# One list schedule for two MLPs and the gating unit between them, with the fourth Winograd product one stage later

## The chip, the cores and the metric

The kernel runs on one core of a Trainium2 chip. The metric is device time in microseconds (us): the median of several executions. Beside it stands one profiled execution, whose trace gives the start and length of each instruction. Engines are named as in the profile: PE multiplies matrices (PEld loads its weights), DVE and ACT do elementwise work, POOL issues the accumulating transfers and small scalar work, SP issues the other transfers.

## The reference

A decoder of two layers, 512 tokens, width 1024, everything in float32. Cut to what matters:

```python
for i in range(2):
    sh1, sc1, g1, sh2, sc2, g2 = jnp.split(silu(c) @ ada_w[i] + ada_b[i], 6, axis=-1)
    h = modulate(rmsnorm(x, norm_mix_g[i]), sh1, sc1)
    y = pool_mixer(h, ...) if i == 0 else sgu_mixer(h, ...)
    x = x + g1[:, None, :] * y
    h = modulate(rmsnorm(x, norm_mlp_g[i]), sh2, sc2)
    x = x + g2[:, None, :] * (jnp.square(jax.nn.relu(h @ mlp_w1[i])) @ mlp_w2[i])   # 1024 -> 4096 -> 1024
return rmsnorm(x, final_g)

def sgu_mixer(h, w_in, ln_g, ln_b, w_s, b_s, w_out):      # the gating unit of layer 1
    u, v = jnp.split(gelu(h @ w_in), 2, axis=-1)
    v = layernorm(v, ln_g, ln_b)
    mixed = einsum('hts,bnshc->bnthc', tril(w_s), v in chunks of 128) + b_s
    return (u * mixed) @ w_out
```

## The kernel before, in words

**Numbers.** Each float32 operand is split in two halves of lower precision: ACT writes the high part (`wh`, or the first half of `hb`, `as`, `op`), DVE subtracts it and writes the low part (`wl`, ...). A product is three matmuls: low weights by high data, high by low, high by high (`mm3`). So each 128x1024 weight tile costs ACT one copy, DVE one subtraction, and the two must be done before PE reaches it.

**Both MLPs by Winograd.** The first matrix (w1) is taken in 8 column quads (c, j), c from 0 to 3, j from 0 to 1. Some columns are done plainly (units `f`); the rest, 5 quads of MLP 0 and 7 of MLP 1, take 7 products of block sums instead of 8 (units `s`, products m = 1 to 7). The sums of weight blocks are made in one buffer, tile `tr` (tag `t0` in pool `hx`), as a chain: block (0,0) is loaded and split for m=1, DVE adds a block and it is split for m=5, again for m=6, then POOL issues a transfer that adds block (1,0) in flight, and the result is split for m=4. A product takes 24 matmuls. The order in a quad is 1 5 6 3 7 2 4 (`ORDER`); the first quad of MLP 1 takes 1 2 5 6 3 7, then m=1 of the next quad, then its own 4. Results are evicted to tiles `g` (pool `gq`, 8 buffers); m=4 adds to the PSUM bank that m=1, 6 and 7 have used, so it has to wait until DVE has read m=7 out of it (`g<-g,po`).

The second matrix (w2) goes the same way in units `p` (m, c): `ORDER2`. Its weight sums are chains in tiles `bt`, one for each c, in the homes `HOME`; the additions are transfers that POOL issues (`sum_in`), and its left operands are `op` tiles. The first unit is m=1, c=0.

**The gating unit** in between uses pools of its own (`lp`, `up`, `gp`, `ur`), opened after those of MLP 0 are closed and closed before those of MLP 1 are opened.

**What sets the order.** PE's order is that of the code. A class `Plan` records the instructions of an MLP, then gives out each engine's in an order that a list scheduler finds: it walks a clock, costs each instruction (`cost`), ranks what is ready by how late it may be (`late`), and emits in order of planned start. Costs and lead times are numbers in the code. MLP 0 and MLP 1 are each planned alone (`LEAD`, `LEAD1`); between them the order of DVE and ACT, and of the transfers, comes from the tile framework. An engine executes strictly in the order given: whatever stands behind an instruction that waits, waits too. This holds for SP too, where a transfer waits for its buffer. In the profile the lines tell who emitted: L130 is the plan's, L102 is everything else.

Names: `raw` are weight tiles as loaded (tag `w4`, 3 buffers), `yr` other blocks of the w1 quads, `yb` and `b` blocks of w2, `h32` (short `h` in the profile) the normalized input in float32, `hb` its split halves, `as` split sums of it, `xs` token rows scaled by their norm, `px` their transposes, `ada` weights of the modulation, worked off on DVE beside the rest.

Of the kernel before, what the change touches and what calls it, by code (L numbers as in the profile page):

```python
# [14 lines left out]
P = 128  # L15
D = 1024
# [60 lines left out]
class Plan:  # L77
# [68 lines left out]
    def cost(name, attr, out, ins, kw):  # L146
# [3 lines left out]
        if attr == "dma_start":  # L150
            mb = out[0].free_size() * out[0].partition_size() / 2**18
            return (5.05 * mb, 3.6 + 4.8 * mb) if kw.get("accum_op") else (2.7 * mb, 0.9 + 5.2 * mb)
        if name == "PE":
            n = out[0].free_size()
            t = max((n + 6) / 2400, 0.1117) if ins[0].dtype == F32R else 2 * max((n + 6) / 2400, 0.1055)
            return t, t + 0.165
        if name == "DVE":
            t = n / 960 + 0.065
            return t, t + 0.09
        if name == "ACT":  # L160
            t = n / 1200 + (0.05 if psum else 0.095)
            return t, t + 0.112
        return (0.75, 0.8) if n < 4 else (n / 950 + 0.1, n / 950 + 0.12)
# [39 lines left out]
    def run(self, lead):  # L203
# [37 lines left out]
        for i in range(N - 1, -1, -1):  # L241
            x = min([late[j] - cost[j][1] for j in succs[i] if j > i], default=t + 20)
# [53 lines left out]
        events, now, free, queue = [], 0.0, {e: lead[e] for e in ready}, 0.0  # L296
# [8 lines left out]
        while count < N:  # L305
            moved = True
            while moved:
                moved = False
                for e in ready:
                    if free[e] > now + 1e-9 or e == "SP" and queue > now + self.QUEUED:  # L310
                        continue
# [24 lines left out]
                    if ops[i][1] == "dma_start":  # L336
                        issue = 0.85 if e == "POOL" else 0.35
                        free[e] = now + issue
                        queue = max(queue, now + issue) + cost[i][0]
                        end = max(queue + 1.8, now + cost[i][1]) + 0.7  # L340
                        heapq.heappush(events, (queue - self.QUEUED + 0.01, -1))
                    else:
                        free[e] = now + cost[i][0]
                        end = now + cost[i][1]
                    heapq.heappush(events, (free[e], -1))
                    heapq.heappush(events, (end, i))
# [11 lines left out]
            now, i = heapq.heappop(events)  # L358
# [25 lines left out]
def decoder_kernel(ctx: ExitStack, tc: tile.TileContext, xtok, vecs, fgrow, ada0, ada1, pool_w, w1s, w1, w1f, w1b, w2, w_v, w_u, w_o, wsT, lnp, bs, out):  # L384
# [233 lines left out]
    ordered = ExitStack()  # L618
    ordered.enter_context(tc.manual_schedule(engines={mybir.EngineType.DVE, mybir.EngineType.Activation, mybir.EngineType.SP}))
# [402 lines left out]
    def mlp(i, first, extra, last, ending):  # L1022
# [3 lines left out]
        with (  # L1026
            tc.tile_pool(name="gq", bufs=8) as gq_,
            tc.tile_pool(name="hx", bufs=1) as hx_,
            tc.manual_schedule(engines=ORDERED | ({mybir.EngineType.DVE, mybir.EngineType.Activation, mybir.EngineType.SP} if i and PLAN[1] else set())),
        ):  # L1030
            gq, hx = (plan.pool(p, True) for p in (gq_, hx_))
            plan.on = PLAN[i]
            shift(hx, BASE)
# [98 lines left out]
            def s_prep(u):  # L1132
# [65 lines left out]
            HOME = ((hx, "hx"), (hx, "t0"), (big, "hb00"), (big, "hb10"))  # L1198
# [18 lines left out]
            def block_at(c, r, n):  # L1217
# [7 lines left out]
                elif (c, n) == (2, 1):  # L1225
# [13 lines left out]
            def p_prep(u):  # L1239
# [31 lines left out]
                if m in (1, 5):  # L1271
# [64 lines left out]
            at = len(units)  # L1336
# [35 lines left out]
            if plan.on:  # L1372
# [342 lines left out]
```

## Time and profile before

| | us |
|---|---|
| median of 3 executions (lowest, highest) | 807.11 (806.63, 807.22) |
| the profiled execution, its own time | 808.29 |
| its span, first to last instruction | 806.6 |
| PE busy | 786.3 (97%) |
| DVE busy | 681.1 (84%) |
| ACT busy | 505.0 (63%) |

The stages, by the trace: pooling mixer and the first 7 column blocks of MLP 0 up to 92 us (not planned), w1 of MLP 0 up to 213, w2 up to 360, gating unit up to 496, w1 of MLP 1 up to 656, w2 up to 799, and the end. PE's granted clock is full in nearly all of them (mean 0.999). "Busy" of PE joins matmuls that overlap in its pipeline, so that a pause of less than a matmul's length does not show as idle.

### The profile page before, as it was taken

The page shows a single profiled execution, that of the slowest core. Times are in us where ns is not written, and L with a number is a line of the kernel's source. Part 1 is how long each engine was busy: PE and PEld are TensorE (multiplying, and loading weights), DVE is VectorE, ACT ScalarE, POOL GpSimd, SP SyncE. Part 2 cuts the span into 40 slices and gives each one's busy share as a digit, 9 for nine tenths or more (in the row PEclk, how much of TensorE's full clock was granted, in tenths as well). Part 3 has the DMA queues.
Part 4 walks back from the last instruction along what each step waited for, and adds up shares of the span by engine and source line. Part 5 has one row for each costly group of instructions (what it writes and reads, how often), then busy time and mean ns, then how long its engine had stood idle before and what let it go on. Part 6 is the DMA issues. An engine that isn't in the chain of part 4 may idle for free.

```text
span 806.6 us, 12583 instructions
## 1 busy us (share of the span) xinstructions
PE 786.3 (97%) x4868; PEld 712.8 (88%) x4868; DVE 681.1 (84%) x883; ACT 505.0 (63%) x723; POOL 85.7 (11%) x110
## 2 busy tenths in 40 slices
PE   5999999999999999999999999999999999999996
PEld 5778889999988888888889889999999998888885
DVE  5989798899879997996898976878877987888897
ACT  5486686577756665776334236767776776666662
POOL 4000000010011131010010001001000011113102
PEclk9999999999999999999999999999999999999999
DMA  8989968786999999126756647366776499999802
GB/s 344 417 304 312 348 211 284 248 275 187 337 291 222 236 258 256 67 100 257 243 184 215 216 145 281 134 183 210 195 200 207 137 352 253 265 239 206 220 1 104
DMA packets 46955, 184.40 MB, mean 229 GB/s; under 512 B 5272, under 2 KB 5424, under 8 KB 42672
## 3 DMA queue, kind: packets, MB, share of 16 engines
q1 hardware_dynamic: 36432, 129.33, 43.2%
q0 software_dynamic: 10032, 51.92, 30.7%
q10 hardware_dynamic: 432, 2.36, 0.7%
q8 instruction: 38, 0.62, 0.3%
q14 instruction: 21, 0.17, 0.1%
HBM read 177.28 MB, written 6.30 MB: 228 GB/s over the span
## 4 chain that ended last, share of the span: by engine, by line
PE 87%; DVE 5%; DMA 5%; issue 1%; ACT 1%; SPq 1%; POOLq 0%; DVEq 0%; ACTq 0%
PE pm L130 36%; PE po L130 29%; PE po L102 18%; DMA ada<-in_ada 2%; PE px L102 1%; DMA tr<-in_w1b 1%; DMA x<-in_xtok 1%; PE pq L102 1%; DVE ada L102 1%; DMA raw<-in_w1f 1%; DVE wl L130 1%; DVE wl L102 1%; DVE tr L130 0%; PE pt L102 0%; DVE ht L102 0%
## 5 line engine op out<-in xcount | busy, mean ns | idle before, releaser
L130 PE MATMUL pm<-wh,op 128*128 128x512 f32 x896 | 267.3, 379 | 0.0
L130 PEld LDWEIGHTS pm<-wh,op 128*128 128x128 f32 x896 | 169.3, 189 | 24.1
L130 PE MATMUL po<-hb,wh 128*128 128x256 f32 (+1 forms) x976 | 173.6, 284 | 0.2 <-DVE hb L130 0.2
L130 PE MATMUL pm<-wl,op 128*128 128x512 f32 x448 | 169.8, 379 | 0.0
L130 PEld LDWEIGHTS po<-hb,wh 128*128 128x128 f32 x976 | 150.0, 192 | 2.6 <-DVE hb L130 0.4
L130 PE MATMUL po<-hb,wl 128*128 128x256 f32 (+1 forms) x489 | 136.3, 284 | 2.8 <-DVE g L130 2.2
L130 PE MATMUL po<-as,wh 128*128 128x256 f32 x576 | 97.1, 275 | 0.0
L130 PEld LDWEIGHTS po<-hb,wl 128*128 128x128 f32 x489 | 92.5, 192 | 4.4 <-DVE g L130 2.5
L130 ACT ACTIVATE op<-g 128x1024 fp32r<-128x1024 f32 x56 | 59.3, 1059 | 58.9 <-PE pm L130 52.5
L130 PEld LDWEIGHTS pm<-wl,op 128*128 128x128 f32 x448 | 84.7, 189 | 11.9
L130 DVE TENSOR_TENSOR op<-g,op 128x1024 fp32r<-128x1024 f32 x56 | 68.5, 1223 | 27.2 <-ACT op L130 27.2
L130 PEld LDWEIGHTS po<-as,wh 128*128 128x128 f32 x576 | 87.5, 192 | 0.0
L130 ACT ACTIVATE g<-g 128x512 f32<-128x512 f32 x100 | 60.4, 627 | 31.4 <-DVE g L130 30.5
L130 DVE TENSOR_TENSOR wl<-bt,wh 128x1024 fp32r<-128x1024 f32 x64 | 77.5, 1220 | 2.1 <-ACT wh L130 1.9
L130 PE MATMUL po<-as,wl 128*128 128x256 f32 x288 | 79.3, 275 | 0.0
L130 ACT ACTIVATE wh<-bt 128x1024 fp32r<-128x1024 f32 x64 | 67.0, 1053 | 15.2 <-PE pm L130 13.6
L130 DVE TENSOR_TENSOR wl<-tr,wh 128x1024 fp32r<-128x1024 f32 x48 | 57.9, 1222 | 20.6 <-ACT wh L130 20.5
L102 PE MATMUL po<-hb,wh 128*128 128x512 f32 x240 | 71.6, 380 | 0.0
L130 ACT ACTIVATE wh<-tr 128x1024 fp32r<-128x1024 f32 x48 | 49.9, 1057 | 17.9 <-DVE tr L130 9.9
L102 DVE SCALAR_TENSOR_TENSOR ada<-ada,cb 128x1024 f32<-128x1024 f32 x42 | 50.9, 1220 | 7.6 <-DMA ada<-in_ada 7.4
L130 PEld LDWEIGHTS po<-as,wl 128*128 128x128 f32 x288 | 55.3, 192 | 0.2 <-ACT g L130 0.2
L102 PEld LDWEIGHTS po<-hb,wh 128*128 128x128 f32 x240 | 45.1, 189 | 6.7 <-DVE hb L102 0.6
(216 smaller groups left out, 1259.0 us busy)
## 6 DMA issues: line engine op xcount, KB each, us to landing
ada<-in_ada SPq DMA_DIRECT2D x76, 512.0 KB, 4.9
bt<-in_w POOLq DMA_DIRECT2D x24, 1024.0 KB, 10.8
yr<-in_w1b SPq DMA_DIRECT2D x22, 512.0 KB, 5.8
b<-in_w SPq DMA_DIRECT2D x20, 512.0 KB, 8.5
bt<-in_w SPq DMA_DIRECT2D x16, 512.0 KB, 9.6
tr<-in_w1b SPq DMA_DIRECT2D x12, 512.0 KB, 4.6
raw<-in_w1b SPq DMA_DIRECT2D x12, 512.0 KB, 5.6
wh<-in_ada SPq DMA_DIRECT2D x10, 512.0 KB, 9.7
```

What stands on the lines that cost most here:

```text
L102: return f(*a, **kw)
L130: self.ops.append((name, attr, lambda: f(*a, **kw), out, ins, kw))
```

## The change

Matmuls and their number stay the same. What differs:

1. **One plan.** `plan.on` is set once, before MLP 0, and `plan.run(LEAD)` is called once, at the end. The gating unit and both seams between stages are thereby ordered by the list scheduler too. Pools `gq` and `hx` are opened once for all three; the gating unit's tiles (`lnt`, `wsbs`, `u`, `gt`) are `g` buffers, `ur` is the home `hx`, and the scaled rows `xs` are a `g` buffer at the first seam and the home `t0` at the second, instead of two `w4` buffers. One of each two `xs` rows is scaled on DVE in every case (before: only in one of four).
2. **m=4 one stage later**, behind m=1 of the next quad, in every quad; in the last quad behind the first unit `p`. Its chain's last addition is a transfer in every quad (before, in the last quad DVE made it). The first two `op` operands now lie in `x0` and `x1`, homes are reordered, and block (1,1) of c=0 is added to its chain by DVE instead of by a POOL transfer.
3. **The planner's numbers.** Costs of transfers, short float32 matmuls, instructions with an accumulator and DVE's scaling change; transfers of different engines share the DMA engines in the plan's clock by row size, and at most 6 wait per queue.

```diff
-LEAD = dict(SP=0.0, POOL=0.0, ACT=9.0, DVE=9.0, PE=13.0, fresh=7.0, wait=1.5, look=0)
-LEAD1 = dict(SP=0.0, POOL=0.0, ACT=9.0, DVE=9.0, PE=10.0, fresh=7.0, wait=3.0, look=16)
-PLAN = (True, True)
+LEAD = dict(SP=0.0, POOL=0.0, ACT=9.0, DVE=9.0, PE=13.0, fresh=7.0, wait=.5, look=16)
...
-            return (5.05 * mb, 3.6 + 4.8 * mb) if kw.get("accum_op") else (2.7 * mb, 0.9 + 5.2 * mb)
+            t = (5.2 if kw.get("accum_op") else 4.0 if out[0].space == bass.MemoryType.DRAM else 2.6) * mb
+            return t, t + 3.0
...
-            x = min([late[j] - cost[j][1] for j in succs[i] if j > i], default=t + 20)
+            rest = 0 if any(tag[x].startswith("hb") for x in self.tiles[i]) else 5
+            x = min([late[j] - cost[j][1] for j in succs[i] if j > i], default=t + rest)
...
+        def flow(t):
+
+            nonlocal moved_to
+            heads = [q[0] for q in lines.values() if q]
+            for x in heads:
+                x[0] -= (t - moved_to) * x[1] / sum(y[1] for y in heads)
+            moved_to = t
...
-        with (
-            tc.tile_pool(name="gq", bufs=8) as gq_,
-            tc.tile_pool(name="hx", bufs=1) as hx_,
...
-            plan.on = PLAN[i]
...
-                if m == 4 and (c, j) == (3, 1):
-                    V.tensor_tensor(t, t, b(*CHAIN[4]), ALU.add)
                 wb = b(1, 1) if m == 3 else b(1, 0) if m == 2 else b(0, 1) if m == 7 else t
                 w = split(wb)
-                if m == 6 and (c, j) != (3, 1):
+                if m == 6:
                     add(t, *CHAIN[4])
...
-            HOME = ((hx, "hx"), (hx, "t0"), (big, "hb00"), (big, "hb10"))
+            HOME = ((hx, "hx"), (big, "hb00"), (hx, "t0"), (big, "hb10"))
...
-                if not n:
-                    pool, tag = big, "x0"
+                if n < 2:
+                    pool, tag = big, f"x{n}"
                 elif m == 4 and c > 1:
-                    pool, tag = HOME[c - 2]
+                    pool, tag = HOME[2 * c - 4]
...
-                elif (c, n) == (2, 1):
+                elif (c, n) in ((0, 0), (2, 1)):
                     t = [w4.tile([P, D], F32, name="raw", tag="w4") for q in range(2)]
...
-                if m in (1, 5):
+                if (c, m) == (0, 5):
+                    for q in range(2):
+                        V.tensor_tensor(b[q], b[q], kept[0][q], ALU.add)
+                elif m in (1, 5):
                     sum_in(chain[c], c, *CHAIN[m + 4 if m == 1 else 6])
...
-            if FROM[i] < 3 - i:
-                units[at + 6 : at + 8] = units[at + 7], units[at + 6]
             units += [("p", (int(u[1]), int(u[0]))) for u in ORDER2.split()]
+            for n in at:
+                units[n : n + 2] = units[n + 1], units[n]
...
+        if not hf:
+            xs_[:] = [hx.tile([P, 2, D], F32, name="xs", tag="t0") if h32 else gq.tile([P, 2, D], F32, name="xs", tag="g")]
         for r in range(2):
-            t = w4.tile([P, D], F32, name="xs", tag="w4")
+            t = xs_[0][:, r]
...
-        xs = xs or scaled_rows(hf)
+        xs = xs or scaled_rows(hf, True)
...
+    us = [gq.tile([P, 4, S], F32, name="u", tag="g") for _ in range(2)]
+    gts = [[gq.tile([P, 4, S], F32R, name="gt", tag="g") for _ in range(2)] for _ in range(2)]
+    ur = hx.tile([P, 2, D], F32, name="ur", tag="hx")
...
     mlp(1, first1, ex, last1, lambda: None)
+    plan.run(LEAD)
```

**Where the order moves.** First place: DVE at the end of the second quad of MLP 0. `po` are PSUM results, `g` the evicted ones, `wl<-tr` the low parts of the chain. Before:

```order
L130 TENSOR_TENSOR wl_1043<-tr_994,wh_1042 128x1024
L130 TENSOR_TENSOR wl_1045<-tr_994,wh_1044 128x1024
L130 TENSOR_TENSOR g_1023<-po_1027,g_1023 128x512
L130 TENSOR_TENSOR tr_994<-tr_994,yr_997 128x1024
L130 TENSOR_TENSOR g_1023<-g_1023,po_1024 128x512
```

With the change:

```order
L128 TENSOR_TENSOR wl_1043<-tr_994,wh_1042 128x1024
L128 TENSOR_TENSOR mods0_89<-pmv_1024,vec_78 128x2
L128 TENSOR_TENSOR tr_994<-tr_994,yr_997 128x1024
L128 TENSOR_TENSOR wl_1047<-tr_994,wh_1046 128x1024
L128 SCALAR_TENSOR_TENSOR ada_1036,pmv_1037<-ada_1036,cb_103 128x1024
L128 TENSOR_TENSOR g_1019<-po_1027,g_1019 128x512
L128 TENSOR_TENSOR wl_1051<-tr_994,wh_1050 128x1024
L128 SCALAR_TENSOR_TENSOR ada_1065,pmv_1062<-ada_1065,cb_103 128x1024
L128 TENSOR_TENSOR g_1019<-g_1019,po_1020 128x512
```

Before, the split for m=4 (`wl_1043`) stands ahead of the reading of m=3 and m=7 (the two `g` rows). Now `wl_1043` is the split for m=1 of the next quad, which needs no accumulated block; the split for m=4 is `wl_1047`, and PE asks for it one product later.

Second place: SP at the seam between the gating unit and w1 of MLP 1. Before:

```order
L130 DMA raw_4761<-in_w1f 128x1024
L130 DMA tr_4781<-in_w1b 128x1024
L130 DMA rg_4754<-in_w1b 128x1024 x2
L130 DMA tr_4781<-in_w1b 128x1024
L130 DMA raw_4764<-in_w1f 128x1024
L130 DMA raw_4784<-in_w1b 128x1024
```

With the change:

```order
L128 DMA raw_1519<-in_w1f 128x1024
L128 DMA raw_1522<-in_w1f 128x1024
L128 DMA raw_1540<-in_w1b 128x1024
L128 DMA raw_1568<-in_w1b 128x1024
L128 DMA raw_1589<-in_w1b 128x1024
L128 DMA tr_1537<-in_w1b 128x1024 x2
L128 DMA raw_1611<-in_w1b 128x1024
```

The fourth plain column block (`raw_4764`, now `raw_1522`) stands ahead of `tr`; both blocks of `tr`, which now share their buffer with `xs`, stand behind four more weight tiles.

Third place: SP at the start of w2 in MLP 0. Before:

```order
L130 DMA ada_1111<-in_ada1 128x1024
L130 DMA bt_1119<-in_w2 128x1024 x2
L130 DMA yb_1143<-in_w2 128x1024 x2
L130 DMA bt_1137<-in_w2 128x1024 x2
L130 DMA b_1127<-in_w2 128x1024 x2
```

With the change:

```order
L128 DMA ada_1111<-in_ada1 128x1024
L128 DMA yb_1144<-in_w2 128x1024 x2
L128 DMA raw_1217<-in_w2 128x1024
L128 DMA bt_1117<-in_w2 128x1024 x2
L128 DMA ada_1134<-in_ada1 128x1024
```

The weights of the first unit `p` (`bt_1119`, now `bt_1117`) were first and are now behind three loads; `raw_1217` takes the `w4` buffer of the last quad's m=2 weights (`raw_1105`).

More of the change, by code (lines that the diff above doesn't have):

```diff
@@ L295, in run, with landing @@
                 soon[ops[j][0]].add(j)
-        events, now, free, queue = [], 0.0, {e: lead[e] for e in ready}, 0.0
+        events, now, free = [], 0.0, {e: lead[e] for e in ready}
+        lines, moved_to, epoch = {e: [] for e in ready}, 0.0, 0
+        def flow(t):
[4 more added lines that the diff above has]
+            moved_to = t
+        def landing():
+            nonlocal epoch
+            epoch += 1
+            total = sum(q[0][1] for q in lines.values() if q)
+            ends = [(q[0][0] * total / q[0][1], e) for e, q in lines.items() if q]
+            if ends:
+                w, e = min(ends)
+                heapq.heappush(events, (max(now, now + w), -2, epoch, e))
         for e in (*ready, "fresh"):
@@ L309, in run @@
                 for e in ready:
-                    if free[e] > now + 1e-9 or e == "SP" and queue > now + self.QUEUED:
+                    if free[e] > now + 1e-9 or e == "SP" and sum(x[0] for x in lines[e]) > self.QUEUED or len(lines[e]) > 6:
                         continue
@@ L338, in run @@
                         free[e] = now + issue
-                        queue = max(queue, now + issue) + cost[i][0]
-                        end = max(queue + 1.8, now + cost[i][1]) + 0.7
-                        heapq.heappush(events, (queue - self.QUEUED + 0.01, -1))
+                        flow(now)
+                        row = min(x.free_size() for x in (*ops[i][3], *ops[i][4]))
+                        lines[e].append([cost[i][0] + 0.01, cost[i][0] * min(1, 2048 / row), i])
+                        landing()
+                        end = now + cost[i][1] + sum(x[0] for x in lines[e][:-1])
                     else:
```

230 lines of the change are left out of this document (115 added, 115 removed).

## The prediction

> **What bounds the kernel now.** I read the page first.
>
> ```profile
> span 806.6 us, 12583 instructions
> PE 786.3 (97%) x4868; PEld 712.8 (88%) x4868; DVE 681.1 (84%) x883; ACT 505.0 (63%) x723; POOL 85.7 (11%) x110
> PE 87%; DVE 5%; DMA 5%; issue 1%; ACT 1%; SPq 1%; POOLq 0%; DVEq 0%; ACTq 0%
> ```
>
> PE is the bound: 97% busy, 87% of the chain that ended last. The change leaves PE its matmuls, so only PE's pauses can move the time. Where they lie is told by the windows, each row a stretch: its bounds, length, busy time of PE, PEld, DVE, ACT and POOL with counts, PE's granted clock, DMA share, GB/s.
>
> ```profile
> 0.00:92.00 92.00, 82.60 (x486) 65.85 (x487) 76.40 (x163) 56.17 (x122) 10.21 (x21) 1.00 0.93 347
> 150.00:160.00 10.00, 9.08 (x81) 8.89 (x81) 9.97 (x14) 6.68 (x10) 0.86 (x1) 1.00 0.66 196
> 160.00:354.00 194.00, 194.00 (x1135) 176.47 (x1135) 174.53 (x194) 130.56 (x156) 26.17 (x30) 1.00 0.82 223
> 520.00:541.00 21.00, 19.78 (x176) 19.42 (x174) 17.71 (x18) 14.08 (x19) 1.78 (x2) 1.00 0.69 193
> 541.00:654.00 113.00, 112.97 (x1010) 112.96 (x1011) 88.20 (x95) 80.34 (x120) 8.58 (x10) 1.00 0.67 200
> 799.00:806.60 7.60, 0.00 (x1) 0.00 (x0) 3.38 (x7) 1.99 (x3) 0.86 (x1) 0.85 0.37 138
> ```
>
> Up to 92 us PE idles 9.4, and in the tail 7.6; the order of all engines is the same there before and after, so I count nothing. In between PE idles in few places: 0.92 us in 150 to 160, 1.22 in 520 to 541, none in 160 to 354, 0.03 in 541 to 654. The stretch 541 to 654 gives the undisturbed pace: 112.97 us for 1010 matmuls, 0.112 each, 2.68 for a product of 24. The waits of PE from 92 to 800 us (PE's work, awaited work, us in total, times, longest) name them all, 3.3 us in five waits:
>
> ```profile
> PE po L130 <- DVE g L130: 2.2, 2, 1.2
> PE po L130 <- DVE wl L130: 0.6, 1, 0.6
> PE po L102 <- DVE hb L102: 0.3, 1, 0.3
> PE po L130 <- DVE hb L130: 0.2, 1, 0.2
> ```
>
> Idle time understates a pause, since the last matmul's pipeline covers some of it. I measure a loss from one start to the next, less the pace.
>
> **The change, part by part.** *m=4 one stage later.* The timeline (start, length, engine, line, operation, count, idle before and who ended it) shows the two waits for `g`:
>
> ```profile
> 139.46 0.86 POOL L130 DMA_DIRECT2D tr<-in_w1b  x1 [6.05 <-DVE wl L130]
> 148.53 2.03 ACT L130 ACTIVATE wh<-tr 128x1024 fp32r<-128x1024 f32 x2 [2.49 <-DMA tr<-in_w1b]
> 149.62 2.36 DVE L130 TENSOR_TENSOR wl<-tr,wh 128x1024 fp32r<-128x1024 f32 x2 [3.03 <-ACT wh L130]
> 153.06 0.39 PE L130 MATMUL po<-hb,wh 128*128 128x256 f32 x2
> 154.37 0.38 PE L130 MATMUL po<-hb,wl 128*128 128x256 f32 x1 [0.92 <-DVE g L130]
> 526.93 0.90 POOL L130 DMA_DIRECT2D tr<-in_w1b  x1 [24.62 <-DVE wl L130]
> 536.33 2.03 ACT L130 ACTIVATE wh<-tr 128x1024 fp32r<-128x1024 f32 x2 [3.23 <-DMA tr<-in_w1b]
> 539.39 0.39 PE L130 MATMUL po<-hb,wh 128*128 128x256 f32 x2
> 541.03 0.38 PE L130 MATMUL po<-hb,wl 128*128 128x256 f32 x1 [1.25 <-DVE g L130]
> ```
>
> In both, POOL's accumulating transfer lands 9.1 and 9.4 us after its issue; DVE, in order, stands idle before `wl<-tr` (3.03 us in the first), is late with the `g` rows behind it, and m=4 of PE waits for the last of these. Two matmuls and the gap from 153.06 to 154.37 are 1.31 us where pace gives 0.22: 1.1 lost; from 539.39 to 541.03, 1.64 less 0.22: 1.4 lost. In the new order (first place shown) the accumulated split stands ahead of those `g` rows no longer: the DVE rows ahead are a split of an old block and short work, and PE has one more product of 2.68 us before it asks. First pause: gain 1.1 of 1.1. In MLP 1's first quad the m=4 split was already one product late and still stalled; what can shrink it is the transfer's start. Its `yr` loads go now later than the transfer, not just ahead of it. But one addition of 1.22 us has come ahead of the m=7 reading. I take 1.0 of 1.4, between 0.2 (only the addition counts) and all.
>
> *Gating unit and second seam.* In the gating unit PE waits at
>
> ```profile
> 372.01 0.60 PE L102 MATMUL px<-ident,xs 128*128 128x128 f32 x4
> 372.94 0.48 PE L102 MATMUL po<-wh,hb 128*128 128x512 f32 x1 [0.33 <-DVE hb L102]
> 497.63 0.36 SPq L130 DMA_DIRECT2D raw<-in_w1f  x1
> 505.19 1.23 DVE L130 TENSOR_TENSOR wl<-raw,wh 128x1024 fp32r<-128x1024 f32 x1 [4.03 <-ACT wh L130]
> 505.57 0.39 PE L130 MATMUL po<-hb,wh 128*128 128x256 f32 x2
> 506.56 0.35 PE L130 MATMUL po<-hb,wl 128*128 128x256 f32 x1 [0.60 <-DVE wl L130]
> ```
>
> The first, 372.94 less 372.01 against 0.44 for four matmuls of 128 columns, loses 0.5; the transposes and `hb` can now be ordered ahead by the scheduler. Gain 0.4 (from 0 to 0.5). At the seam the fourth plain block was loaded at 497.63, its buffer held by `xs`; its split came at 505.19 and PE lost 0.99 less 0.22, 0.8. DVE's backlog behind it gives the wait for `hb` of 0.2 above, 0.3 by pace. In the new order (second place shown) this load is one row behind the third, and `xs` is no longer in its buffers: gain 1.0 of 1.1. Sum of gains: 1.1 + 1.0 + 0.4 + 1.0 = 3.5.
>
> *What the seam adds.* The two loads of `tr` share a buffer with `xs`, and so wait until the last transpose has read it:
>
> ```profile
> 503.71 1.91 PE L130 MATMUL px<-ident,xs 128*128 128x128 f32 x16
> 511.78 1.22 DVE L130 TENSOR_TENSOR wl<-tr,wh 128x1024 fp32r<-128x1024 f32 x1
> tr<-in_w1b SPq DMA_DIRECT2D x12, 512.0 KB, 4.6
> 506.50:534.20 27.70, 27.47 (x240) 27.07 (x241) 26.75 (x28) 20.75 (x31) 0.90 (x1) 1.00 0.49 157
> ```
>
> The transposes end at 505.6. Three weight tiles stand ahead of `tr` on SP, the third in the buffer of the fourth plain block, which the split of 505.19 frees at 506.4 at the latest. Issue is thus at 505.6 to 506.4; with the median landing of 4.6 us data is there at 510.2 to 511.0. ACT's split takes 1.06 (2.03 for two above), so DVE can begin at 511.3 to 512.1, against 511.78 before: cost 0.2. Nothing on SP behind these loads is needed sooner. The dear end is a rival below.
>
> *Starts of w2.* The first unit `p` comes one product, 2.68 us, sooner, and its weights `bt` stand behind `yb` and `raw_1217` on SP (third place shown):
>
> ```profile
> 201.73 1.22 DVE L130 TENSOR_TENSOR wl<-raw,wh 128x1024 fp32r<-128x1024 f32 x1
> 200.22 0.80 SPq L130 DMA_DIRECT2D bt<-in_w  x2
> 204.35 1.06 ACT L130 ACTIVATE wh<-bt 128x1024 fp32r<-128x1024 f32 x1
> 206.93 1.06 ACT L130 ACTIVATE wh<-bt 128x1024 fp32r<-128x1024 f32 x1 [1.52 <-DMA bt<-in_w]
> 213.43 0.38 PE L130 MATMUL pm<-wh,op 128*128 128x512 f32 x1
> bt<-in_w SPq DMA_DIRECT2D x16, 512.0 KB, 9.6
> ```
>
> `raw_1217` takes the buffer that the split at 201.73 frees at 202.95; at 0.4 us an issue `bt` goes at 203.4, three us later than at 200.22. Before, the two blocks were there within 4.1 us (ACT began at 204.35) and 6.7 us (206.93). With 4.1 the splits (1.06 + 1.22) end at 209.8, with 6.7 at 212.4; PE asks at 213.43 less 2.68, 210.75. So the stall is 0 to 1.6; at 9.6, the median over both stages, it would be 4.5, but there four and more loads stand in SP's queue, and here three. I take 0.6, nearest the middle of 4.1 and 6.7 (0.3) with something for the second block. MLP 1 starts w2 in the same order, so twice: 1.2. SP's `ada` behind `bt` is awaited by no product here. The additional accumulating transfer in the last quad has, beside it, a product of `p` for cover.
>
> The Trainium skill, page "DMA: Bandwidth & Descriptors", section "Queues, rings and completion order", says that each DMA engine takes turns, packet by packet, between the queues it has work for. By that rule the accumulating transfer on POOL's queue would take every second packet beside SP's `bt` loads, and the first of these would land later by one 512 KB tile: by an estimate from the 417 GB/s that the page of the profile shows at most, 1.25 us, so that the two starts would cost up to 2.4 more and the time be about 807.4. The landings of 9.1 and 9.4 us against 4.6 point that way; no row shows it at this place.
>
> *Work that I cost at nothing.* Some `xs` rows move from ACT to DVE, two additions in each w2 start move from POOL's transfers to DVE (1.22 us each), and two additions leave DVE. Between 160 and 354 DVE is idle for 19.5 of 194 us while PE doesn't pause: that hides them. Without that cover each would cost its 1.22. The planner's numbers only matter through the order.
>
> **Sum.** Gains 3.5, costs 0.2 + 1.2 = 1.4, net 2.1. The profiled execution has a span of 806.6 and its own time of 808.29; the median of the runs is 807.11, 1.18 lower. On the median 807.1 - 2.1 = 805.0.
>
> **The rivals.** *All pauses go, nothing new comes.* The losses sum to 1.1 + 1.4 + 0.5 + 1.1 = 4.1: 803.0. For it: half of `tr`'s loads land within 4.6 us, and the first `bt` within 4.1. Against: DVE at 26.75 of 27.70 us where it must also do more.
>
> *The starts of w2 give the gain back.* With the 6.7 us landing each start costs 1.6, not 0.6: 807.0, no change. For it: three loads ahead in one queue. Against: the split that frees `raw_1217`'s buffer may go sooner than 202.95.
>
> *The change doesn't do what it says*: the orders shown exclude that m=4 stays put; the second wait for `g` may stay, though, without its 1.0: 806.0. I count it with the forecast's spread.
>
> *Slower: `tr` at the second seam.* If its loads land as late as the worst shown, 9.4 us, after 506.4, the data is there at 515.8, DVE's split starts at 516.9, 5.1 late, and DVE, strictly in order, stands. The chain of additions behind it ends in the split for m=6:
>
> ```profile
> 525.41 1.22 DVE L130 TENSOR_TENSOR wl<-tr,wh 128x1024 fp32r<-128x1024 f32 x1
> 525.98 0.28 PE L130 MATMUL po<-as,wl 128*128 128x256 f32 x1
> ```
>
> It is done at 526.63, and m=6 starts one product after 525.98, at 528.66: a slack of 2.0, with DVE 97% busy, and the added addition (1.22) and `xs` row may eat that too. PE is late by 3.1 to 5.1: 808.1 to 810.1, middle 809.1. It decides once `tr` lands about 3 us behind its median. For it: two loads behind three in the queue. Against: all `tr` loads of SP have a median of 4.6.
>
> **How the numbers follow.** Forecast 805.0, between 803.8 and 806.2: 0.45. All pauses go, 803.0: 0.12. No change, 807.0: 0.20. Slower, 809.1: 0.23, with `bt` at 9.6 in it. 0.2%, or 1.6 us, is about what a measurement can tell: faster is below 805.5, slower above 808.7. Of the forecast about a ninth lies above 805.5: faster 0.40 + 0.12 = 0.52, same 0.25, slower 0.23. The range reaches from 802.4 (the first rival and the runs' own 0.6) to 809.4, past the middle of the last.
>
> **What would show it.** In the changed kernel's waits no PE wait for `g` near 153, one of at most 0.4 us near 540, none for `wl` near 506; `wl<-tr` starting at 511 to 512; and the first `pm` product 2 us sooner in its stage, with an idle time ahead of 0 to 1 us. The prediction is wrong if PE waits for `wl` at either start of w2 by more than 1.6 us, if the first `wl<-tr` after the seam comes behind 514, or if idle time appears inside 160 to 354 or 541 to 654, where it was under 0.05.

## The result, and the profile after

| | kernel before | changed |
|---|---|---|
| median of 21 executions each, taken side by side (lowest, highest) | 808.59 us (806.63, 812.05) | 804.57 us (803.04, 807.46) |
| the profiled execution, own time | 808.29 | 807.26 |
| its span | 806.6 | 805.2 |

The ratio is 0.9949, 95% interval 0.9936 to 0.9962: about 4.1 us faster, clear of no change. The forecast was 805.0 and a gain of 2.1. The time was met, the gain was not: it is twice as large, and the two times agree by luck, because the median of 807.11 from which I subtracted, of three executions, lies 1.5 us below that of 21.

One execution of either kernel differs from the next by some us, and of the two profiled ones only that of before, 808.29, lies near its median: the changed kernel's, 807.26, is nearly its slowest. So the spans alone, 806.6 and 805.2, would have told too little. This is why both kernels were profiled a second time below.

The page of the changed kernel:

```profile
span 805.2 us, 12574 instructions
PE 786.2 (98%) x4868; PEld 712.0 (88%) x4868; DVE 685.8 (85%) x888; ACT 504.9 (63%) x718; POOL 83.6 (10%) x110
```

PE's busy time is the same within 0.1 us, as it had to be. Its waits from 92 to 800 us (PE's work, awaited work, us in total, times, longest):

```profile
PE po L128 <- ACT g L128: 1.5, 2, 0.9
PE pm L128 <- DVE wl L128: 0.4, 1, 0.4
```

The five waits of before are all gone, 3.3 us in sum; 1.9 us of others have come. Windows (bounds, length, busy time of PE, PEld, DVE, ACT, POOL with counts, PE's clock, DMA share, GB/s) show where the old ones were:

```profile
150.00:160.00 10.00, 10.00 (x92) 10.00 (x91) 9.48 (x15) 7.59 (x11) 0.85 (x1) 1.00 0.80 234
490.00:520.00 30.00, 30.00 (x249) 29.36 (x248) 25.27 (x35) 21.36 (x35) 3.10 (x3) 1.00 0.50 174
520.00:541.00 21.00, 20.11 (x180) 19.92 (x179) 19.14 (x20) 15.41 (x21) 1.81 (x2) 1.00 0.64 176
```

The second of these stretches, in the kernel before:

```profile
490.00:520.00 30.00, 29.22 (x237) 28.15 (x235) 24.03 (x36) 22.35 (x38) 1.62 (x3) 1.00 0.58 214
```

In 150 to 160 and in 490 to 520 PE doesn't pause any more (before it was busy 9.08 of 10.00 and 29.22 of 30.00). In 520 to 541 a new pause stands, and the timeline says what it is:

```profile
531.46 1.07 ACT L128 ACTIVATE wh<-tr 128x1024 fp32r<-128x1024 f32 x1 [2.69 <-DMA tr<-in_w1b]
532.42 1.28 ACT L128 ACTIVATE g<-g 128x512 f32<-128x512 f32 x2
533.61 0.58 ACT L128 ACTIVATE g<-po 128x512 f32<-128x512 f32 x1
534.24 0.38 PE L128 MATMUL po<-hb,wl 128*128 128x256 f32 x1 [0.89 <-ACT g L128]
```

ACT, in order, stands 2.69 us at the split for m=4, until the accumulating transfer has landed. Behind it stand two rows on `g` and the reading of a PSUM bank (`g<-po`), and PE waits for that bank. It is the old stall on another engine. The prediction had followed DVE there and not ACT. The other wait for ACT's `g`, 0.6 us at 125, is not of this kind: ACT works without a gap there from 118.10 on, after it had stood 2.17 us for an addition of DVE to `tr`.

At the first start of w2 the wait that I had expected is there:

```profile
200.60 1.62 SPq L128 DMA_DIRECT2D bt<-in_w  x2
209.40 1.06 ACT L128 ACTIVATE wh<-bt 128x1024 fp32r<-128x1024 f32 x1 [2.47 <-DMA bt<-in_w]
211.77 0.48 PE L128 MATMUL pm<-wl,op 128*128 128x512 f32 x1 [0.36 <-DVE wl L128]
```

### The profile page after: what moved, and what is told of

The parts are those of the page before. It is cut to its first block, busy times and chain, and to the rows that moved or that the text cites. A ratio compares the mean times of both kernels' runs of the same rounds, so it can differ in the third digit from the quotient of the medians.

```text
span 805.2 us, 12574 instructions
## 1 busy us (share of the span) xinstructions
PE 786.2 (98%) x4868; PEld 712.0 (88%) x4868; DVE 685.8 (85%) x888; ACT 504.9 (63%) x718; POOL 83.6 (10%) x110
## 4 chain that ended last, share of the span: by engine, by line
PE 79%; DMA 9%; DVE 5%; issue 4%; ACT 2%; SPq 0%; POOLq 0%; POOL 0%; DVEq 0%; ACTq 0%
PE po L128 40%; PE pm L128 36%; DMA ada<-in_ada 3%; DMA raw<-in_w 1%; DMA wh<-in_ada 1%; DVE wl L128 1%; DMA bt<-in_w 1%; DMA x<-in_xtok 1%; ACT wh L128 1%; DVE ada L100 1%; PE po L100 1%; DMA yr<-in_w1b 1%; DMA tr<-in_w1b 1%; PE pq L100 0%; PE px L128 0%
## 5 line engine op out<-in xcount | busy, mean ns | idle before, releaser
L128 PE MATMUL po<-hb,wh 128*128 128x256 f32 (+1 forms) x1104 | 211.3, 295 | 0.0
L128 PEld LDWEIGHTS po<-hb,wh 128*128 128x128 f32 x1104 | 174.2, 191 | 5.5
L128 PE MATMUL po<-hb,wl 128*128 128x256 f32 (+1 forms) x553 | 160.9, 296 | 0.9 <-ACT g L128 0.9
L128 PEld LDWEIGHTS po<-hb,wl 128*128 128x128 f32 x553 | 104.6, 191 | 4.1 <-ACT g L128 1.1
L128 DVE TENSOR_TENSOR wl<-raw,wh 128x1024 fp32r<-128x1024 f32 (+1 forms) x52 | 60.6, 1176 | 14.4 <-ACT wh L128 14.4
L128 DVE SCALAR_TENSOR_TENSOR ada<-ada,cb 128x1024 f32<-128x1024 f32 x56 | 67.9, 1217 | 5.1 <-DMA ada<-in_ada 5.1
L128 ACT ACTIVATE wh<-raw 128x1024 fp32r<-128x1024 f32 (+1 forms) x52 | 51.6, 1004 | 28.5 <-PE po L128 11.9
```

Of the source, the lines that this page charges most:

```text
L128: self.ops.append((name, attr, lambda: f(*a, **kw), out, ins, kw))
```

## The experiments

All ran in three sets and one single run, each with its own runs of the kernel before on the same chip. The ratios are to these. The last column is PE's waits between 92 and 800 us in the profiled execution, summed from that view.

| kernel | median us (executions) | ratio, 95% interval | PE waits, us |
|---|---|---|---|
| before | 808.59 (21) | | 3.3 |
| before, second trace | 810.61 (1) | | 4.8 |
| m=4 moved, alone | 807.71 (12) | 0.9995, 0.9972 to 1.0018 | 3.0 |
| two DVE rows exchanged, alone | 807.78 (12) | 0.9975, 0.9953 to 0.9998 | 1.3 |
| changed | 804.57 (21) | 0.9949, 0.9936 to 0.9962 | 1.9 |
| changed, second trace | 804.75 (10) | 0.9950, 0.9932 to 0.9967 | 0 |
| changed, m=4 not moved | 808.09 (12) | 0.9991, 0.9973 to 1.0010 | 5.6 |
| changed, three plans | 817.39 (4) | 1.0091, 1.0065 to 1.0118 | 7.8 |
| changed, old numbers | 808.38 (12) | 0.9984, 0.9969 to 0.9999 | 4.2 |
| changed, `xs` in `w4` | 808.47 (12) | 0.9988, 0.9971 to 1.0004 | 3.6 |
| changed, last quad's m=4 not moved | 806.04 (12) | 0.9967, 0.9955 to 0.9980 | 2.7 |
| m=4 not moved, transfer reckoned 3 us longer | 806.33 (8) | 0.9959, 0.9940 to 0.9977 | 2.3 |
| changed, transfer reckoned 3 us longer | 803.32 (6) | 0.9930, 0.9911 to 0.9949 | 0 |
| changed, transfer reckoned 2 us longer | 804.89 (7) | 0.9951, 0.9933 to 0.9969 | 0.5 |

A trace is one execution and can lie far from the median: that of the exchanged rows (805.52) is the fastest of its twelve, those of m=4 not moved (811.33) and of the last quad's m=4 not moved (807.77) are among the slowest of theirs.

My theory going in: the gain is the five pauses, some taken away by moving m=4, some by the common schedule. The rivals: that it lies in the stretch up to 92 us or in the single execution; that moving m=4 is most of it; that the planner's numbers are.

**The changed kernel again.** No edit.

> The changed kernel, not edited. Theory (the five pauses of PE after 92 us carried the gain): a second trace shows the new pauses at about 124, 211 and 533 us again, each within 0.4 us of its 0.8, 0.5 and 1.1, none for g at 153 or 540 and none at 506; the time is 0.4 to 0.6% below the kernel before. Rival (the gain lies in the stretch up to 92 us, or is a matter of the single execution): pauses after 92 us differ by over 1 us from one trace to the other, and the last matmul of the stretch up to 92 us comes over 1.5 us sooner than in the kernel before.

The time is as expected, the pauses aren't. The second trace has no wait of PE between 92 and 800 us at all. At the same place in MLP 1:

```profile
523.43 0.94 POOL L128 DMA_DIRECT2D tr<-in_w1b  x1 [22.08 <-DVE wl L128]
525.42 1.93 SPq L128 DMA_DIRECT2D yr<-in_w1b  x4
528.53 1.06 ACT L128 ACTIVATE wh<-tr 128x1024 fp32r<-128x1024 f32 x1 [1.40 <-DMA tr<-in_w1b]
```

The transfer landed 5.1 us after its issue (5.4 in the first trace), ACT stood 1.40 instead of 2.69, and the bank was read in time. So the new pauses of the first trace belong to that execution. Half of the rival was right: pauses differ by over 1 us from one execution to the next. The other half was wrong: the span fell to 802.5 although the last two matmuls of the first stretch, the one up to about 92 us, begin at 92.70, before at 92.11.

**The kernel before again.** No edit.

> The kernel before, not edited, for a second trace. Theory: the pauses at 153, 372, 506, 511 and 540 us are there again, each within 0.4 us of its 1.1, 0.5, 0.8, 0.3 and 1.4. Rival: pauses elsewhere after 92 us, of over 1 us in all, which the first trace did not have; then the first trace understated what the change could take away.

```profile
PE po L130 <- DVE wl L130: 1.4, 1, 1.4
PE po L130 <- DVE g L130: 1.3, 1, 1.3
PE pm L130 <- ACT wh L130: 0.8, 1, 0.8
PE pm L130 <- DVE wl L130: 0.8, 1, 0.8
PE po L102 <- DVE hb L102: 0.3, 1, 0.3
PE po L130 <- DVE hb L130: 0.2, 1, 0.2
```

The pauses at the gating unit, the seam and the first quad of MLP 1 came back; that for `wl` at the seam was 1.4, not 0.6. The pause at 153 us did not: its transfer was split by ACT 6.5 us after its issue, not 9.1. Two waits in w2 came, 0.8 each, which the first trace didn't have. Waits of 3.3 and 4.8 before against 1.9 and 0 after: 3.1 us less on average, and the mean of the two spans fell from 807.8 to 803.9, by 3.9, close to the measured 4.1. It lies where the plan works: from the last two matmuls of the first stretch to the last of w2 it is 706.5 and 709.2 us before, 704.5 and 701.9 after, 4.7 less on average; the first stretch is 0.8 longer, and the tail 8.0 in all four. The pipeline covers part of each pause, so the waits say less than the spans. The first trace of before had understated what there was to take away.

**Moving m=4, alone.** In the kernel before:

```diff
-            at = len(units)
+            at = []
...
+                at += [len(units) - 1] if q < 7 else []
-            if FROM[i] < 3 - i:
-                units[at + 6 : at + 8] = units[at + 7], units[at + 6]
...
+            for n in at:
+                units[n : n + 2] = units[n + 1], units[n]
```

> The kernel before, with m=4 one stage later in every quad but the last; its two plans, pools and numbers stay. Theory: the pause at 153 us (1.1 us) goes, those at 372, 506, 511 and 540 (0.5, 0.8, 0.3, 1.4) stay: 1.1 us faster than before, ratio 0.9986. Rival (moving m=4 is most of the change): 3 us or more faster, ratio 0.9963 or less. Rival (an order made for the old units gives the gain back): no change, a new wait for g or wl of about 1 us in its place.

Ratio 0.9995, its interval includes no change and 1.1 us alike, but not 3 us. The two large waits that stayed:

```profile
PE po L130 <- DVE g L130: 1.5, 1, 1.5
PE po L130 <- DVE wl L130: 1.0, 1, 1.0
```

The pause at 153 us is absent here, but it is absent from the second trace of before too. Under the old plans moving m=4 is worth 0.28%, 2.3 us, at most by this interval. The rival that it is most of the change falls, in this form.

**m=4 not moved, in the changed kernel.**

```diff
-                at.append(len(units) - 1)
+                at += [len(units) - 1] if q == FROM[i] < 3 - i else []
...
+                if m == 4 and (c, j) == (3, 1):
+                    V.tensor_tensor(t, t, b(*CHAIN[4]), ALU.add)
...
-                if m == 6:
+                if m == 6 and (c, j) != (3, 1):
```

> The changed kernel with m=4 at its old place in every quad but MLP 1's first, and DVE's addition in the last quad as before; one plan and its numbers stay. Theory: it loses the 1.1 us of the second quad and gains the 0.5 of the first start of w2, so that it is 0.3 to 1 us slower than the changed kernel, about 0.4% faster than before; no pause at 506 and 511. Rival (one schedule orders DVE well enough without it): no wait for g over 0.3 us, and not slower than the changed kernel. Rival (moving m=4 is most): within 0.2% of before.

The time, 0.9991, is that of the last rival, moving m=4 is most: nearly the whole gain is lost. But its reading doesn't fit the run before this one, where the same move gained nothing by itself. The largest wait shows why (ACT first, then PE):

```profile
123.19 0.57 ACT L128 ACTIVATE g<-po 128x512 f32<-128x512 f32 x1
128.09 1.06 ACT L128 ACTIVATE wh<-tr 128x1024 fp32r<-128x1024 f32 x1 [4.33 <-DMA tr<-in_w1b]
129.05 0.58 ACT L128 ACTIVATE g<-po 128x512 f32<-128x512 f32 x1
129.68 0.38 PE L128 MATMUL po<-as,wl 128*128 128x256 f32 x1 [2.92 <-ACT g L128]
```

The planner has put the split of the accumulated block ahead of the bank's reading; the transfer, issued at 120.99, took 7.1 us, and ACT stood for 4.33. So m=4 one stage later and the common plan with its numbers are not two terms to be added: the new plan needs the later m=4, and the old plans hardly gain by it.

**Three plans instead of one.**

```diff
     mlp(0, first0, sorted(ex, key=lambda x: x[0]), gated, ending0)
+    plan.run(LEAD)
+    plan.on = True
...
     fgb = []
+    plan.run(LEAD)
+    plan.on = True
```

> The changed kernel with its plan run three times: behind MLP 0, behind the gating unit and at the end; buffers, m=4 and numbers as changed. If the common schedule carries the gain: the wait for wl or hb at the seam near 506 comes back with 0.8 to 1.6 us, and the time is 2 us or more above the changed kernel, ratio to before 0.9975 or more. If the buffers carry it (xs no longer in w4, so that the fourth plain block is loaded early, and the first accumulating transfer of MLP 1 ahead of the yr loads): no pause over 0.4 us at the seam, none for g near 540, ratio 0.995 as with the changed kernel.

The case of the common schedule, far beyond its 2 us and at another wait: slower than before by 0.9%. The largest waits of PE, and ACT at the first seam:

```profile
PE po L128 <- ACT wh L128: 5.9, 2, 3.2
PE po L128 <- DVE wl L128: 1.1, 1, 1.1
```

```profile
361.99 0.63 ACT L128 ACTIVATE tmp<-x 128x512 f32<-128x512 f32 x1 [2.67 <-DVE x L128]
362.52 0.19 ACT L128 ACTIVATION_READ_ACCUMULATOR tmp<-x 128x1 f32 x1
362.62 2.93 ACT L128 ACTIVATE wh<-raw 128x1024 fp32r<-128x1024 f32 x3
```

The last squares of one stage wait for DVE, and the first weight splits of the next stand behind them, because a plan gives out all of its instructions before the next begins. The other seam shows the same at 505. The common plan has these splits ahead. The waits, 7.8 us, are not the whole loss: behind the two largest the trace shows a lower granted clock, 0.50 in 365 to 370 and 0.58 in 508 to 511, and at the first of them matmuls of 512 columns start 0.43 us apart instead of 0.22. Each of the three plans starts from the lead times made for one; what others would give was not run. In this kernel, with its buffers, it is worth the distance from 1.0091 to 0.9949. That isn't the share of the gain by which the common plan beats the kernel before, where the gating unit was not planned at all and the seams were ordered by the tile framework.

**The planner's old numbers.** Costs, lead times and the one common queue of the kernel before, in the changed kernel (the edit is the third part of the change taken back; its `LEAD`):

```diff
-LEAD = dict(SP=0.0, POOL=0.0, ACT=9.0, DVE=9.0, PE=13.0, fresh=7.0, wait=.5, look=16)
+LEAD = dict(SP=0.0, POOL=0.0, ACT=9.0, DVE=9.0, PE=13.0, fresh=7.0, wait=1.5, look=0)
```

> The changed kernel with the planner's costs, lead and model of the queues as before (wait 1.5, look 0, one common queue, a last instruction's lateness of 20). If the numbers matter only through few rows: ratio to before 0.995, the pauses of the changed kernel at 124, 211 and 533 us at most 1 us in all. If they matter (the old ones reckon an accumulating transfer 1.5 us longer): the waits for g of ACT behind an accumulated split go, but new ones of 1 us or more come at w2 or in the gating unit, which these numbers were not made for; ratio 0.997 to 1.0.

The second case, nearly as written: 0.9984, with new waits in the gating unit (the first two below lie mainly there).

```profile
PE po L128 <- DVE hb L128: 1.5, 2, 1.0
PE px L128 <- DVE xs L128: 0.9, 1, 0.9
PE pm L128 <- DVE wl L128: 0.8, 1, 0.8
```

No wait for ACT's `g` is in this view. The numbers are thus worth as much as moving m=4: without either the kernel is within 0.2% of before, and without the common plan slower.

**The scaled rows in `w4` again.**

```diff
-            t = xs_[0][:, r]
+            t = w4.tile([P, D], F32, name="xs", tag="w4")
```

> The changed kernel with the scaled rows xs in two w4 buffers again, at both seams. Theory (xs in w4 holds up the fourth plain block): its split comes late, PE waits for wl near 506 for 0.6 to 1.6 us, and the time is 0.8 to 2 us above the changed kernel, ratio to before 0.996 to 0.9975. Rival (one schedule loads the block early enough anyway): no wait for wl there, ratio 0.995 or less.

The time goes in the theory's direction, beyond its range (0.9988), but the mechanism is not there: no wait for `wl` at the seam.

```profile
PE po L128 <- ACT g L128: 3.0, 1, 3.0
PE px L128 <- DVE xs L128: 0.4, 1, 0.4
PE pm L128 <- DVE wl L128: 0.2, 1, 0.2
```

```profile
521.68 1.75 SPq L128 DMA_DIRECT2D yr<-in_w1b  x4
523.09 0.93 POOL L128 DMA_DIRECT2D tr<-in_w1b  x1 [21.41 <-DVE wl L128]
533.00 1.06 ACT L128 ACTIVATE wh<-tr 128x1024 fp32r<-128x1024 f32 x1 [3.73 <-DMA tr<-in_w1b]
```

The plan loads the fourth plain block early in any case. What costs is elsewhere: with other buffers the plan issues the four `yr` loads 1.4 us ahead of the accumulating transfer; that lands 9.9 us after its issue, ACT stands 3.73 us, and PE 3.0. So this run speaks for the order of the two, not for the buffer.

**Two rows of DVE exchanged, alone.** The kernel before, `wl` of the m=6 split ahead of the second `as` row. DVE's order in MLP 1's first quad is the only one that differs:

```order
 L130 TENSOR_TENSOR tr_4781<-tr_4781,rg_4754 128x1024
 L130 TENSOR_TENSOR as_4796<-h32_4352,as_4796 128x1024
+L130 TENSOR_TENSOR wl_4790<-tr_4781,wh_4789 128x1024
 L130 TENSOR_TENSOR as_4801<-h32_4352,as_4801 128x1024
-L130 TENSOR_TENSOR wl_4790<-tr_4781,wh_4789 128x1024
 L130 TENSOR_TENSOR wl_4792<-rg_4754,wh_4791 128x1024
```

> The kernel before, with two rows of DVE exchanged and nothing else: in MLP 1's first quad the low part of the m=6 split is made ahead of the second of two as rows. The accumulating transfer, which waits for that split, is thereby issued about 1 us ahead of the four yr loads, which wait for the as row, not 1.4 us behind them. Theory (the transfer lands 9 us after its issue only because four loads stand ahead of it): landing 5 to 6.5 us after the issue, the wait for g near 540 falls from 1.2 to 1.5 us to under 0.4, time 1 to 1.4 us below before, ratio 0.9985. Rival (an accumulating transfer is slow beside loads in any order): landing 8 to 10 us, the wait stays over 1 us, ratio 1.0. Rival (DVE, 97% busy there, is late for m=6 or m=3 by the exchange): a new wait for as or wl of 0.5 us or more between 525 and 532.

```profile
524.53 0.90 POOL L130 DMA_DIRECT2D tr<-in_w1b  x1 [23.71 <-DVE wl L130]
525.42 2.00 SPq L130 DMA_DIRECT2D yr<-in_w1b  x4
```

```profile
DMA to landing us min/median/max: 5.2/5.6/6.7
```

The first are POOL's and SP's issues. The last is the line on tile `tr` between 500 and 545 us, for its three transfers there: none over 6.7 us, where this line said 9.4 at most before (9.6 with m=4 moved, 9.4 in the second trace of before). The transfer issued at 524.53 itself landed after 5.6 us. The largest of PE's waits:

```profile
PE po L130 <- ACT g L130: 0.6, 1, 0.6
```

The wait for DVE's `g`, which all three traces with the old order have (1.2, 1.3, 1.5), is gone; a wait of 0.6 for ACT's `g` has come 9 us sooner, at 530, where none was. So 0.6 us of this trace's 2.0 us of saved waits is the exchange's; the rest, the pause at 153 and part of that at the seam, is missing from this execution for other reasons. One exchange of two rows takes 0.25% off the kernel before, with an interval, 0.02 to 0.47%, that nearly reaches no change. The theory holds for the landing and for the wait that it named, and it is the cleanest of these runs, since no other row is ordered otherwise.

**The last quad's m=4 ahead of w2.**

```diff
-                at.append(len(units) - 1)
+                at += [len(units) - 1] if q < 7 else []
```

> The changed kernel with m=4 of the last quad ahead of the first product of w2 again, in both MLPs; m=4 stays one stage later in the other quads, and its last addition stays a transfer. Forecast of the start of w2 (0 to 1.6 us each, 0.6 taken): no pause at the first product of w2, but m=4 comes one product sooner behind its transfer, which costs 0.5 to 2 us there each time if the landing is 5 us or more; ratio 0.995 to 0.998. Rival (the first product of w2 costs more than m=4): no wait for wl or g at either place, ratio 0.9935 to 0.9945.

0.9967, as the forecast had it, and not for its reason:

```profile
208.76 1.06 ACT L128 ACTIVATE wh<-bt 128x1024 fp32r<-128x1024 f32 x1 [3.96 <-DMA bt<-in_w]
209.85 1.23 DVE L128 TENSOR_TENSOR wl<-bt,wh 128x1024 fp32r<-128x1024 f32 x1 [3.80 <-ACT wh L128]
210.99 0.68 DVE L128 TENSOR_TENSOR g<-g,po 128x512 f32<-128x512 f32 x1
211.73 0.38 PE L128 MATMUL po<-hb,wl 128*128 128x256 f32 x1 [2.67 <-DVE g L128]
```

m=4 waits for the reading of m=7, and that stands on DVE behind the split of `bt`, whose load is late. m=4's own transfer is not what is awaited. With m=4 behind the first product of w2, PE asks for `bt` itself, and a like lateness (ACT began its split 8.8 and 8.0 us after the issue, here 10.3) cost 0.4 and 0 us. Here too the loss is more than the wait: in 214 to 216 us the granted clock is 0.50, and matmuls of 256 columns start 0.21 us apart instead of 0.11.

**A longer reckoned transfer.** Several of these runs point to one place: the planner takes an accumulating transfer to be there 2.6 us of transfer plus 2.0 after its turn, 4.6 where no other queue shares the engines with it, and orders ACT and DVE by that. On the chip those looked at here took 5.1 to 9.9.

```diff
-                heapq.heappush(events, (now + 2.0, lines[more[1]].pop(0)[2]))
+                x = lines[more[1]].pop(0)[2]
+                heapq.heappush(events, (now + (5.0 if ops[x][5].get("accum_op") else 2.0), x))
```

In the changed kernel:

> The changed kernel, but its planner reckons that the data of an accumulating transfer are there 5 us after it has had the queues, not 2 (7.6 us in all, as the landings of 7 and 9 us on the chip ask for). ACT's split for m=4 then stands behind the reading of the bank that PE waits for (g<-po) in MLP 1's first quad. Theory (what is left in the changed kernel's slower executions is ACT standing at that split): no wait for ACT's g over 0.3 us at 124 and 533 us, highest time of the runs under 806, median 0.5 to 1 us below the changed kernel, ratio 0.9935 to 0.995. Rival (the new numbers put other rows late): new waits of 1 us or more, ratio 0.996 or more.

As the theory has it, with a little more gain than its range: no wait of PE between 92 and 800 us in its trace, and 803.32, ratio 0.9930. The highest of its six executions is 805.80, within the bound of 806 that was set. Its interval overlaps that of the changed kernel, 0.9936 to 0.9962, so that it is faster than before for certain, and faster than the changed kernel by the medians only. The traces don't show that last difference either: from the last two matmuls of the first stretch to the last of w2 it is 701.85 us here and 701.85 in the second trace of the changed kernel. The 1.4 us between their spans lie in the first stretch (91.31 against 92.70), where both have the same order. What the run shows is that the waits for ACT's `g` are absent; the second trace of the changed kernel lacks them too, so whether the new number keeps them away in every execution is not shown.

With m=4 not moved:

> The changed kernel with m=4 at its old place, as before, and with the planner's 5 us for an accumulating transfer. It tells why m=4 at its old place had lost the whole gain under one plan. If it lost it because the plan reckons the transfer too short and puts ACT's split ahead of the g rows: the wait of 2.9 us near 126 and that of 1.3 near 551 fall under 0.5 each, ratio 0.995 to 0.997. If m=4 has no time at its old place however the rows stand: PE waits for wl of that split instead, 1 us or more in several quads, ratio 0.998 to 1.001.

```profile
PE po L128 <- DVE hb L128: 1.0, 1, 1.0
PE po L128 <- DVE g L128: 0.9, 1, 0.9
PE po L128 <- DVE wl L128: 0.4, 1, 0.4
```

The waits for ACT's `g` are gone, 5.6 us of waits become 2.3, and the ratio goes from 0.9991 to 0.9959. So the transfer reckoned too short explains a part of what m=4 at its old place had lost. The move still counts under the longer reckoning: 0.9959 without it against 0.9930 with it, a distance of 0.3%, where it was 0.4% under the old one (0.9991 against 0.9949). The intervals are too wide to tell these two distances apart.

With 4.0 in place of 5.0, in the changed kernel:

> As the run in which the planner reckoned 5 us behind the queues for an accumulating transfer, but with 4 us: in MLP 0 ACT's rows are now nearly those of the changed kernel (the m=4 split still ahead of the read that PE waits for), in MLP 1's first quad the split stands behind it. If the order of that split is the mechanism, the wait for ACT's g near 533 is gone and one near 124 of up to 0.8 us can still be there; ratio to before between 0.993 and 0.995. If the gain of the 5 us was luck of one order, ratio 0.995 or more with waits elsewhere.

0.9951, no better than the changed kernel: just outside the bound, and by its letter the case of luck, with a wait elsewhere; the interval, 0.9933 to 0.9969, holds both cases. No wait for ACT's `g` in its trace, one of 0.5 us for `wl` at the first start of w2. The order of the split alone is thus not all that 5.0 changed; how much of its 0.9930 is order, how much the rows at the start of w2 and how much chance is not settled by these runs.

## Why the prediction was right or wrong

**The size.** I summed one execution's pauses, and took 3.5 of 4.1 us as gain and 1.4 as cost. The pauses of before are larger in other executions (waits of 4.8 against 3.3), and the costs mostly did not come. The nearest case is the first rival, all pauses gone: 4.1 us, which is what the ratio says, and one of two traces shows it outright.

**m=4 one stage later, "gain 1.1 of 1.1".** This is the step that failed. The pause at 153 us is in one of the three traces that have this order in MLP 0 (two of before, one with the rows exchanged): the same transfer, behind the same rows, landed after 9.1, 5.7 and 5.6 us. So the pause was worth less than 1.1 in the mean; alone the move gives 0.9995, with an interval that excludes neither nothing nor 1.1. That the move also keeps PE out of the way of late splits in the new plan (0.9991 without it) I had not seen, since I added the parts.

**MLP 1's first quad, "1.0 of 1.4".** Right in its cause, the transfer ahead of the `yr` loads: the exchange of two rows shows it by itself. All of the wait for DVE's `g` went, not 1.0. A wait for ACT's `g` of up to 0.9 took its place in one execution, zero in the other.

**The gating unit, "0.4 of 0.5".** The four transposes and the next product now start 0.62 apart:

```profile
372.92 0.60 PE L128 MATMUL px<-ident,xs 128*128 128x128 f32 x4
373.54 0.48 PE L128 MATMUL po<-wh,hb 128*128 128x512 f32 x1
```

0.62 less 0.44 is a loss of 0.2, where 0.93 less 0.44 was lost: 0.3 gained, in this trace.

**The seam, "1.0 of 1.1".** Both waits are gone in both traces, and since the second trace of before waited 1.4 + 0.2 there, the gain is larger. The reason that I gave, `xs` no longer in `w4`, isn't supported: with `xs` back there the wait did not return.

**What the seam adds, 0.2, and the slower rival.** `tr` was issued as reckoned (505.6 to 506.4 forecast), but its split began 1.1 us behind the forecast's 511.3 to 512.1, since ACT could start on it only 5.8 us after the issue, not 4.6:

```profile
506.30 0.92 SPq L128 DMA_DIRECT2D tr<-in_w1b  x2
513.20 1.23 DVE L128 TENSOR_TENSOR wl<-tr,wh 128x1024 fp32r<-128x1024 f32 x1 [1.07 <-ACT wh L128]
```

In the second trace it began at 510.55. DVE stood 1.07 us in the slower case and PE did not wait. The 514 that the prediction names as its limit was not reached.

**The starts of w2, "0.6, twice".** Near in one start of four: 0.4 us of wait and 0 in the first stage, 0 in the second in both traces, so that 1.2 in sum was too much by 0.8 to 1.2. Where it was near, two errors cancel: the loads went at 200.60, not 203.4, because the buffer ahead came free sooner (my own argument against the second rival); and ACT could begin on `bt` 8.8 us later, not 5.4, nearer the 9.6 that I had set aside. The rule of the Trainium skill, page "DMA: Bandwidth & Descriptors", section "Queues, rings and completion order", that a DMA engine takes turns between the queues it has work for, does not explain this late landing. The accumulating transfer on POOL's queue, issued at 195.23, landed 5.0 us later, before `bt` was issued, and the 807.4 reckoned by that rule (twice its 1.25 is 2.5, not 2.4) did not come. Four other loads of 512 KB had gone out on SP from 197.24 on; whether they made `bt` late no run separates.

**Costs put at nothing.** Fair for DVE's additional work. Wrong for the planner's numbers "only through the order": through the order they decide some 0.3% (0.9984 with the old). And the prediction followed no ACT row behind an accumulated split, though its own rule, "whatever stands behind an instruction that waits, waits too", covers ACT as well. That wait, 0.9 us at 534 in the profiled execution, had no place in the sum. One sign of being wrong could not tell, either: idle time inside 160 to 354 us, 0.36 in the first trace and none in the second, is the very pause at the start of w2 that the forecast had put at 0.6.

## What to carry to other kernels

Where engines execute in order, the dear instruction is not the late one but what stands behind it: for each transfer that is summed in flight, look on every engine at the row behind its first reader. Parts of a scheduler's change are not terms to be added (without any one of three, two thirds of the gain, nearly all of it or more was gone), so cost the order that comes out, not the edits. And before a sum of pauses below 1% is believed, take a second trace of the same kernel: one of five pauses was absent in the second, and others of 1.6 us had come.

## What the runs showed of the hardware

One accumulating transfer of 512 KB landed 5.1 and 5.4 us after its issue in the changed kernel, where it went 2 us ahead of four loads of 512 KB each (5.6 with the rows exchanged, 0.9 us ahead), and 9.4 to 9.9 us where it went 1.4 us behind them, in four traces (8.8 with the old numbers, 2.8 us behind them). I had that as a guess from one row; the exchange of two instructions moved it from 9.4 to 5.6. Order is not the only cause of a late landing: the transfer ahead of the pause at 153 us took 9.1, 5.7 and 5.6 us in three traces with the same rows around it.

A pause of PE can cost more than its wait. Behind waits of 3.2 and 2.7 us (three plans) and of 2.7 us (last quad's m=4 not moved) the granted clock fell to between 0.50 and 0.58 for some us; behind waits of 2.9 us (m=4 not moved, at 129 us) and 3.0 us (`xs` in `w4`, at 534 us) it stayed at 1.00. These runs don't show what decides it.
